# Low parts of streamed weight pieces: one engine before, two engines after

## The chip, the core and the metric

The kernel runs on one core of a Trainium2 chip. The metric is the time of one execution on the device in microseconds (us). Five engines work side by side, each through its own instructions in a fixed order: TensorE (PE in the profile; PEld is its loading of weights), VectorE (DVE), ScalarE (ACT), GpSimd (POOL) and SyncE (SP, which only issues DMAs here). They wait for each other by semaphores.

## What is computed

Two layers of a hybrid backbone over 256 latent tokens with 256 context tokens, width 1024. Cut to what matters here:

```python
for l in range(2):
    u = rms_norm(h, norm1_g[l]) * (1 + sc1) + sh1          # h: 256 latent (+ 256 context) tokens x 1024
    a_x, a_g, b_q, b_f, b_i, b_o, c_qkv, m_g = split_projection(u @ w_in[l])
    ya = rglru_branch(a_x, a_g, ...)                       # gated linear recurrence, both directions
    yb = hgrn2_branch(b_q, b_f, b_i, b_o, ...)             # state-expanded recurrence, both directions
    yc = neighbourhood_attention(c_qkv, ...)
    h = h + gt1 * (sum_n sigmoid(m_g[n]) * (y_n @ w_branch[l, n])) @ w_out[l]
    h = h + gt2 * sq_relu(modulated_rms_norm(h) @ ffn_w1[l]) @ ffn_w2[l]
```

The context tokens run through the same weights in layer 0; in layer 1 only what the latent tokens read of them is computed. Everything is float32 in and out.

## The kernel before

**Exact products from two parts.** TensorE multiplies in a rounded format. So each float32 operand is split: a high part (the value rounded, written by ScalarE, line 226) and a low part (the value less its high part, line 227), and each product is three matmuls: high by high, high by low, low by high (`mm3`, lines 240 to 242; `mm3_pairs`, 253 to 255; the token-major pieces, 1027 to 1029).

**Weight pieces.** The weights of a layer lie in DRAM as pieces of 128 x 1024, each 512 KB, and are streamed by SyncE into `raw` (three buffers, line 211). `weights` splits a piece into `whi` (ScalarE) and `wlo` (before: VectorE), four buffers of each:

```python
def weights(l, key, raw=None, eng=nc.vector):
    ...
    split(hi, lo, raw, eng=eng)

def split(hi, lo, src, scale=None, eng=nc.vector):
    if scale is None:
        nc.scalar.copy(hi, src)                                                    # line 226
        eng.tensor_tensor(out=lo, in0=src, in1=hi.bitcast(F32), op=ALU.subtract)   # line 227
```

One piece alone (the first, at the start) already has its low part on GpSimd. `fetch` runs ahead: while a piece is multiplied, up to three more are split. With 512 tokens (layer 0) a piece is 24 matmuls of 512 columns, with 256 tokens (layer 1) 24 of 256 columns.

**The order of the pieces** in a layer: four heads with ten pieces each (four token-major `tok` pieces that are multiplied together, then `ff`, `fb`, `hq`, `ax`, `ag`, `og`; the first head of layer 0 has no streamed `tok`), 24 gates and 12 branch projections, eight output pieces (`out`), then the MLP: `f1` (up) and `f2` (down), 32 pieces each. The first four `f1` pieces of an MLP are `("f1", 0, 0)` to `("f1", 0, 3)`. The queue `todo` counts the streamed pieces from 0: heads, merge and MLP of layer 0 are pieces 0 to 143, those of layer 1 pieces 144 to 291; the first four `f1` are 80 to 83 and 228 to 231.

**Work between the matmuls.** The chains of the three mixers (`hgrn`, `attention`, `lru`) are cut into steps that are issued between runs of matmuls. A step is a few VectorE and ScalarE instructions and then matmuls (`lv` line 547, `sc` 746, `pr` and `pi` 847) that need them. In layer 0 VectorE also computes most of the modulation by products of rows (`junk`, line 354).

**The norms.** Before an MLP, and before layer 1, the new residual `h` (line 1145) is squared and summed (`sums`, line 420), summed over the features by TensorE (`nss`, line 429), turned into a reciprocal root by three single-input VectorE steps and seven steps on two inputs (`r_g`, 128 x 2, lines 488 to 490 and 495), spread by TensorE (`rst`, line 443), and applied chunk by chunk: `ut` (line 459, reads `h` and the PSUM tile `rst`), `xhi` (ScalarE, 462) and `xlo` (VectorE, 463, reads `ut` and `xhi`). The next piece's matmuls need `xhi` and `xlo`.

A list scheduler puts each engine's instructions in a row, by its own estimate of when each could run; so an edit on one engine can move others. At run time each row is run as it stands.

Of the kernel before, what the change touches and what calls it, by code (L numbers as in the profile page):

```python
# [56 lines left out]
def merge_order(l):  # L57
    # some gates first, while the mixers' chains end
    count = {}
    for part in MERGE[l].split():  # L60
        bi = int(part[0])
        for what in part[1:]:
            i = count.get((bi, what), 0)
            count[bi, what] = i + 1
            yield bi, BRANCH_ORDER[bi], {"g": "gate", "p": "proj"}[what], i
# [35 lines left out]
class Piece:  # L101
    """Products with streamed weights: body(weights) yields after each run of products."""
# [5 lines left out]
class Lanes:  # L108
    """Chains of dependent steps that are issued between the runs of products.

    A step yields the time that the vector engine needs for what it issued, and how many runs more the chain waits."""
# [43 lines left out]
def hybrid_kernel(  # L155
# [67 lines left out]
    def split(hi, lo, src, scale=None, eng=nc.vector):  # L223
        # hi <- rounded part of scale * src, lo <- the rest
        if scale is None:
            nc.scalar.copy(hi, src)  # L226
            eng.tensor_tensor(out=lo, in0=src, in1=hi.bitcast(F32), op=ALU.subtract)  # L227
        else:
            nc.scalar.mul(hi, src, scale)
            nc.vector.scalar_tensor_tensor(  # L230
                out=lo, in0=src, scalar=scale, in1=hi.bitcast(F32), op0=ALU.mult, op1=ALU.subtract
            )
# [13 lines left out]
    def mm3_pairs(dsts, ws, x, nk, c0, c1):  # L246
        # two pieces at a time, so that x may still be arriving
        for i in range(0, len(dsts), 2):
            for k in range(nk):
                xhi, xlo = (t[:, c0:c1] for t in x(k))  # L250
                for p_, (whi, wlo) in zip(dsts[i:i + 2], ws[i:i + 2]):
                    d = p_[:, c0:c1]
                    nc.tensor.matmul(d, lhsT=whi[:, k, :], rhs=xhi, start=(k == 0), stop=False)
                    nc.tensor.matmul(d, lhsT=whi[:, k, :], rhs=xlo, start=False, stop=False)
                    nc.tensor.matmul(d, lhsT=wlo[:, k, :], rhs=xhi, start=False, stop=(k == nk - 1))
                if k % 2:
                    yield
# [5 lines left out]
    def layer_scalars():  # L263
# [13 lines left out]
        for l in range(DEPTH):  # L277
            # f = lb + (1 - lb) * (1 + tanh) / 2 as offset and slope
# [40 lines left out]
    def rope_tables(l):  # L319
        # ctab[:, cos|sin, tile, k|q, head, :], with the norm's gains and the scores' scale  # L320
        for sc in range(2):
            for i, qk in enumerate((1, 0)):
                g = gf[l][:, 2 * sc + qk, :]
                for hd in range(2):
                    for tt in range(2):
                        nc.gpsimd.tensor_tensor(out=ctab[:, sc, tt, i, hd, :], in0=cst[:, sc, tt, :], in1=g, op=ALU.mult)

# [1 line left out]
    mod = [cpool.tile([P, 3, 2, 16], F32, name=f"mod{l}") for l in range(DEPTH)]  # L329

    def modulation_rows():
        # most sections, a row for each feature: the vector engine has time while the tensor engine is busy
# [34 lines left out]
    def last_modulation():  # L367
        # the last section: four groups of columns in four parts of the array
# [55 lines left out]
    def column_sums(parts, n, tag="A"):  # L424
        # sums over the features, one column for each 128 tokens
# [12 lines left out]
    def spread(r, n, tag="A"):  # L438
        # a row of n * 128 columns in every partition
# [14 lines left out]
    def modulated(u, r, a, b, k, s):  # L454
        # u = h * r * a + b in high and low parts
# [29 lines left out]
    def small_rstd(ss, n, temps):  # L485
        # 1 / sqrt(ss / n + eps) for a few columns: a first guess from the exponent, two steps
# [6 lines left out]
        # with x = v * r * r: r * (15 - 10 x + 3 x^2) / 8, but for the factor 3 / 8, then r * (3 - x) / 2 with that factor  # L493
# [14 lines left out]
    def first_half():  # L508
        # the latent stream's norm, before its products are issued
# [5 lines left out]
    def hgrn(l, j, TF, Q, vtok, sog, ys):  # L515
# [4 lines left out]
        # products over blocks, states of the context stream  # L520
# [9 lines left out]
        # within blocks of 64 tokens, the blocks of a tile side by side  # L530
# [7 lines left out]
        def place(b, src, shift):  # L538
            # blocks in the upper (b = 0) or the lower half of the partitions
# [13 lines left out]
        def mixed(t, hh, c0, n):  # L553
            # [first halves of slot 0 | second halves of slot 1] of the 2*hh blocks in columns c0..c0+n
# [17 lines left out]
        # A^T[s, t] of both directions, level by level  # L572
        Tt = TF[:]
        width = T2
        for lev in range(8):
# [11 lines left out]
            # widen the products to blocks of 2*hh  # L587
# [30 lines left out]
        # final states of the context stream  # L618
# [18 lines left out]
        # outputs, token-major  # L637
# [34 lines left out]
    def attention(l, j, qk, vtok, bias, ys):  # L672
        Tq = T2 if l == 0 else TL
        misc = two_k("misc")
        # normalised keys and queries, token-major: [k | q] of two heads for each 128 tokens
# [23 lines left out]
        # rotary embedding of the latent tokens  # L699
# [48 lines left out]
        def softmax(qt, sc):  # L748
            # both heads at once
# [55 lines left out]
        def applied(qt):  # L805
            # both heads at once, in two parts of the array
# [87 lines left out]
    def fin_query(Tq, Q, p_):  # L894
        # twice the silu
# [5 lines left out]
    def fin_outgate(l, Tq, sog, p_):  # L901
        # the gain over four times (1 + tanh)
# [17 lines left out]
    def fin_gelu(Tq, ge, p_):  # L920
        # twice the tanh GeLU
# [12 lines left out]
    def mixer_pieces(l):  # L934
        T = T2 if l == 0 else TL
        heads = []
        for j in range(4):
# [9 lines left out]
            def opened(nm, m=m, j=j):  # L947
                # tiles of a chain, when its first piece begins
# [9 lines left out]
                if nm == "tok":  # L958
                    m.bias = four_k("bias", (4, TL))
                    (nc.gpsimd if l or j else nc.sync).dma_start(out=m.bias, in_=biasd[l, j])  # L960
                    # [v of both mixers | k and q], two blocks of tokens each
# [28 lines left out]
            def group(ws, m=m, opened=opened, closed=closed):  # L990
                # the first products, while the modulation arrives
# [70 lines left out]
    def merge_pieces(l):  # L1062
# [7 lines left out]
        def gate_tile(bi, d):  # L1070
            # several gates in a tile
# [78 lines left out]
    def down_pieces(l, kind, sub, x, section, T, finished, after, pre=None):  # L1150
        # pieces d = 0..7 into the residual; with after, the last four by streams, so that a norm can start early
# [119 lines left out]
    def start():  # L1271
# [51 lines left out]
        def busy(n):  # L1323
            # keeps the tensor engine's clock up while the first data arrive
# [30 lines left out]
        def arrive():  # L1355
            # what the products of the first chunk need
# [11 lines left out]
        def later():  # L1368
            # what the products of the first chunks don't need
# [11 lines left out]
        def ahead(k, n):  # L1381
            # within the products of chunk k, what those of chunk k + 2 need
# [24 lines left out]
    # weights run ahead of the pieces that use them  # L1407
# [3 lines left out]

    def fetch(n):
        while len(ready) < n and pos[0] < len(todo):
            l, key = todo[pos[0]]
            ready.append(weights(l, key))
# [146 lines left out]
```

## Time and profile before

| | us |
|---|---|
| median of 3 runs | 1526.16 (1526.15 to 1528.68) |
| span of the profiled execution | 1526.3 |
| TensorE busy in it | 1513.7 (99%) |
| VectorE busy | 1115.9 (73%) |
| ScalarE busy | 735.0 (48%) |
| GpSimd busy | 26.4 (2%) |

The profiled execution has a span of 1526.3 us, 0.1 us above the median of the runs, so what its rows add up to can be set against the median directly. [...] A busy TensorE in this profile is one with matmuls in its pipeline; their ends are modelled, so the distance from the start of one matmul to the start of the next tells its rate, and "idle before" tells where it waited.

### The profile page before, as it was taken

How to read it: one execution, taken by the hardware profiler on the slowest of the kernel's cores; microseconds unless marked ns; L12 is line 12 of the kernel's file. 1: busy time of each engine (PE TensorE's matmuls, PEld its weight loads, DVE VectorE, ACT ScalarE, POOL GpSimd, SP SyncE). 2: the span in 40 equal slices, each digit the busy share in tenths (PEclk: the TensorE clock that was granted, in tenths of full speed). 3: DMA queues.
4: the chain of work that ended last, by engine and by line, in shares of the span. 5: the costliest groups of instructions: out<-in, count | busy, mean ns of one | idle time of the engine just before them, and what ended most of it. 6: DMA issues, size and time to landing. Idle time of an engine off the chain costs nothing.

```text
span 1526.3 us, 24145 instructions
## 1 busy us (share of the span) xinstructions
PE 1513.7 (99%) x9554; PEld 1300.8 (85%) x9554; DVE 1115.9 (73%) x2118; ACT 735.0 (48%) x1229; POOL 26.4 (2%) x57
## 2 busy tenths in 40 slices
PE   9999999999999999999999999999999999999999
PEld 4778788878888889888888889888888899999999
DVE  6776768586478898988685856778787856776664
ACT  3457575666333333532322323475766854454442
POOL 0200000020000000000000000000000000000000
PEclk9999999999999999999999999999999999999999
DMA  9413122221273562445463532313313345755553
GB/s 368 146 53 104 56 90 70 70 77 62 91 250 136 187 240 70 171 174 206 139 220 127 204 126 82 133 63 126 104 70 105 109 167 182 274 167 184 186 183 125
DMA packets 61793, 217.36 MB, mean 142 GB/s; under 512 B 7792, under 2 KB 9456, under 8 KB 61680
## 3 DMA queue, kind: packets, MB, share of 16 engines
q1 hardware_dynamic: 59328, 209.88, 39.5%
q0 software_dynamic: 1648, 5.77, 1.2%
q8 instruction: 75, 1.23, 0.3%
q14 instruction: 38, 0.31, 0.1%
q10 hardware_dynamic: 704, 0.17, 0.1%
HBM read 214.74 MB, written 1.05 MB: 141 GB/s over the span
## 4 chain that ended last, share of the span: by engine, by line
PE 96%; DVE 2%; ACT 1%; issue 1%; DMA 0%; SPq 0%; DVEq 0%
PE pd L240 7%; PE pd L242 7%; PE pd L241 7%; PE pf L242 5%; PE pf L240 5%; PE pf L241 5%; PE pg L240 5%; PE pg L241 4%; PE pg L242 4%; PE ptok L1027 3%; PE ptok L1029 3%; PE ptok L1028 3%; PE lv L547 2%; PE pp L241 2%; PE pp L240 2%; PE pp L242 2%
## 5 line engine op out<-in xcount | busy, mean ns | idle before, releaser
L226 ACT CAST whi<-raw 128x1024 fp32r<-128x1024 f32 x296 | 310.3, 1050 | 477.0 <-PE pd L241 157.2
L227 DVE TENSOR_TENSOR wlo<-raw,whi 128x1024 fp32r<-128x1024 f32 x295 | 360.3, 1223 | 151.2 <-ACT whi L226 149.4
L242 PE MATMUL pd<-hhi,wlo 128*128 128x256 f32 (+1 forms) x544 | 177.8, 327 | 0.0
L240 PE MATMUL pd<-hhi,whi 128*128 128x256 f32 (+1 forms) x544 | 177.8, 327 | 0.0
L241 PE MATMUL pd<-hlo,whi 128*128 128x256 f32 (+1 forms) x544 | 177.7, 327 | 0.0
L354 DVE CUSTOM_DVE_ANT_0 junk<-arow,crow 128x1024 bf16<-128x1024 f32 x144 | 173.3, 1219 | 2.2 <-DMA arow<-in_adaw 2.0
L241 PE MATMUL pf<-xlo,whi 128*128 128x256 f32 (+1 forms) x464 | 155.0, 334 | 0.0
L242 PE MATMUL pf<-xhi,wlo 128*128 128x256 f32 (+1 forms) x464 | 155.0, 334 | 0.0
L240 PE MATMUL pf<-xhi,whi 128*128 128x256 f32 (+1 forms) x464 | 155.0, 334 | 0.0
L240 PE MATMUL pg<-xhi,whi 128*128 128x512 f32 (+1 forms) x384 | 131.5, 342 | 0.0
L241 PE MATMUL pg<-xlo,whi 128*128 128x512 f32 (+1 forms) x384 | 129.2, 336 | 0.0
L242 PE MATMUL pg<-xhi,wlo 128*128 128x512 f32 (+1 forms) x384 | 129.2, 336 | 0.0
L1145 DVE SCALAR_TENSOR_TENSOR h<-pd,mod,h 128x256 f32<-128x256 f32 x120 | 54.9, 480 | 81.2 <-PE pd L242 79.2
L241 PEld LDWEIGHTS pd<-hlo,whi 128*128 128x128 f32 x544 | 103.5, 190 | 8.8
L240 PEld LDWEIGHTS pd<-hhi,whi 128*128 128x128 f32 x544 | 103.5, 190 | 8.8
L242 PEld LDWEIGHTS pd<-hhi,wlo 128*128 128x128 f32 x544 | 103.5, 190 | 8.6
L241 PEld LDWEIGHTS pf<-xlo,whi 128*128 128x128 f32 x464 | 88.1, 190 | 8.8
L242 PEld LDWEIGHTS pf<-xhi,wlo 128*128 128x128 f32 x464 | 88.1, 190 | 8.7
L240 PEld LDWEIGHTS pf<-xhi,whi 128*128 128x128 f32 x464 | 88.0, 190 | 8.7
L1027 PE MATMUL ptok<-whi,xhi 128*128 128x512 f32 (+1 forms) x224 | 87.4, 395 | 1.1 <-DVE h L1145 1.1
L1029 PE MATMUL ptok<-wlo,xhi 128*128 128x512 f32 (+1 forms) x224 | 84.4, 377 | 0.0
L1028 PE MATMUL ptok<-whi,xlo 128*128 128x512 f32 (+1 forms) x224 | 84.2, 376 | 0.2 <-DVE xlo L463 0.2
(329 smaller groups left out, 3240.0 us busy)
## 6 DMA issues: line engine op xcount, KB each, us to landing
raw<-in_wpack SPq DMA_DIRECT2D x296, 512.0 KB, 3.5
arow<-in_adaw SPq DMA_DIRECT2D x72, 512.0 KB, 4.7
a<-in_ada0w SPq DMA_DIRECT2D x16, 512.0 KB, 10.4
araw<-in_lastw SPq DMA_DIRECT2D x8, 512.0 KB, 6.3
bias<-in_biasd POOLq DMA_DIRECT2D x7, 512.0 KB, 4.3
h<-in_xT SPq DMA_DIRECT2D x4, 512.0 KB, 5.5
gw<-in_lruw POOLq DMA_DIRECT2D x8, 256.0 KB, 2.9
out<-h SPq DMA_DIRECT2D x8, 128.0 KB, 2.0
```

The costliest lines, as they stand in the source:

```text
L226: nc.scalar.copy(hi, src)
L227: eng.tensor_tensor(out=lo, in0=src, in1=hi.bitcast(F32), op=ALU.subtract)
L240: nc.tensor.matmul(d, lhsT=whi[:, k, :], rhs=xhi, start=(k == 0), stop=False)
L241: nc.tensor.matmul(d, lhsT=whi[:, k, :], rhs=xlo, start=False, stop=False)
L242: nc.tensor.matmul(d, lhsT=wlo[:, k, :], rhs=xhi, start=False, stop=(k == nk - 1))
L354: nc.vector.tensor_tensor_reduce(out=junk, in0=raw, in1=crow[s], scale=1.0, scalar=0.0, op0=ALU.mult, op1=ALU.add, accum_out=section_of(l, ...
L547: nc.tensor.matmul(dst, lhsT=lhs(b), rhs=rhs(b), start=True, stop=True)
L1027: nc.tensor.matmul(dst, lhsT=xhi[:, k, tsl], rhs=whi[:, kk, :], start=(k == 0), stop=False)
L1028: nc.tensor.matmul(dst, lhsT=xlo[:, k, tsl], rhs=whi[:, kk, :], start=False, stop=False)
L1029: nc.tensor.matmul(dst, lhsT=xhi[:, k, tsl], rhs=wlo[:, kk, :], start=False, stop=(k == KD - 1))
L1145: nc.vector.scalar_tensor_tensor(out=h[:, d, sl], in0=p_[:, sl], scalar=mods(l, section, s)[:, d:d + 1], in1=h[:, d, sl], op0=ALU.mult, op ...
```

## The change

The engine of a low part now depends on the place of its piece in the queue: every second piece, and the first four pieces of each MLP, go to GpSimd. Of 292 streamed pieces those are 146 + 4 = 150. The arithmetic is the same.

```diff
     todo = [key for p in pieces for key in p.keys]
     ready = deque()
     pos = [0]
 
+    def low_part_engine(key, i):
+
+        return nc.gpsimd if i % 2 or (key[0] == "f1" and key[1] == 0 and key[2] < 4) else nc.vector
+
     def fetch(n):
         while len(ready) < n and pos[0] < len(todo):
             l, key = todo[pos[0]]
-            ready.append(weights(l, key))
+            ready.append(weights(l, key, eng=low_part_engine(key, pos[0])))
             pos[0] += 1
```

The rest of the diff drops comments and empty lines. In each head GpSimd gets the second and fourth `tok` piece, `fb`, `ax` and `og`.

On GpSimd the low parts stand between its few other instructions, the table `ctab` and the DMA issues of `gw` and `bias`. This is the piece of the difference from the end of head 2 of layer 0 to that of layer 1's first head:

```order
 L968 DMA gw<-in_lruw 128x512
 L960 DMA bias<-in_biasd 128x1024
+L227 TENSOR_TENSOR wlo<-raw,whi 128x1024 x5
+L968 DMA gw<-in_lruw 128x512
+L227 TENSOR_TENSOR wlo<-raw,whi 128x1024
+L960 DMA bias<-in_biasd 128x1024
+L227 TENSOR_TENSOR wlo<-raw,whi 128x1024 x4
+L326 TENSOR_TENSOR ctab<-cst,gf_74 128x64 x16
+L968 DMA gw<-in_lruw 128x512
+L227 TENSOR_TENSOR wlo<-raw,whi 128x1024 x51
```

GpSimd's row is no longer a few set-up steps but low parts throughout, with the DMA issues among them.

On VectorE, at the norm before layer 1's MLP (`r_g` is the reciprocal root, `ut` and `xlo` the normed input), the row before was:

```order
L227 TENSOR_TENSOR wlo<-raw,whi 128x1024
L1145 SCALAR_TENSOR_TENSOR h<-pd,mod_86,h 128x256
L488 TENSOR_SCALAR r_g_12660<-nss 128x2
L489 TENSOR_SCALAR r_g_12660<-r_g_12660 128x2
L490 TENSOR_SCALAR r_g_12660<-r_g_12660 128x2
L495 SCALAR_TENSOR_TENSOR r_g_12660<-r_g_12660 128x2
L227 TENSOR_TENSOR wlo<-raw,whi 128x1024
L495 SCALAR_TENSOR_TENSOR r_g_12660<-r_g_12660 128x2 x6
L459 SCALAR_TENSOR_TENSOR ut<-h,A_g_12671,rst 128x256 x3
L463 SCALAR_TENSOR_TENSOR xlo<-ut,mod_86,xhi 128x256 x3
```

and it is now:

```order
L1145 SCALAR_TENSOR_TENSOR h<-pd,mod_86,h 128x256
L488 TENSOR_SCALAR r_g_12660<-nss 128x2
L489 TENSOR_SCALAR r_g_12660<-r_g_12660 128x2
L490 TENSOR_SCALAR r_g_12660<-r_g_12660 128x2
L495 SCALAR_TENSOR_TENSOR r_g_12660<-r_g_12660 128x2 x7
L459 SCALAR_TENSOR_TENSOR ut<-h,A_g_12671,rst 128x256 x3
L463 SCALAR_TENSOR_TENSOR xlo<-ut,mod_86,xhi 128x256 x3
```

The two low parts that stood before and inside the chain of `r_g` have left VectorE's row; the chain's own steps are the same and stand together. At the norm before layer 0's MLP three low parts leave in the same way, and at the norm before layer 1 one leaves the chain of `r_g` and one the steps behind it.

## Rows read from the trace of the kernel before

**Rows 1.** The page, busy time of the engines (share, instructions).

```profile
PE 1513.7 (99%) x9554; PEld 1300.8 (85%) x9554; DVE 1115.9 (73%) x2118; ACT 735.0 (48%) x1229; POOL 26.4 (2%) x57
```

**Rows 2.** Who TensorE waited for: us in total, times, longest.

```profile
PE pf L253 <- ACT xhi L462: 2.7, 3, 1.1
```

**Rows 3.** Groups by line and form: busy us, mean ns, idle time before.

```profile
L227 DVE TENSOR_TENSOR wlo<-raw,whi 128x1024 fp32r<-128x1024 f32 x295 | 360.3, 1223 | 151.2 <-ACT whi L226 149.4
...
L227 POOL TENSOR_TENSOR wlo<-raw,whi 128x1024 fp32r<-128x1024 f32 x1 | 2.3, 2342 | 11.4 <-ACT whi L226 11.4
```

**Rows 4.** Timeline at the start: start us, us, engine, line, instruction.

```profile
11.62 0.17 DVE L301 TENSOR_TENSOR lq<-lq,lz 128x16 f32<-128x16 f32 x1
...
11.88 2.34 POOL L227 TENSOR_TENSOR wlo<-raw,whi 128x1024 fp32r<-128x1024 f32 x1 [11.44 <-ACT whi L226]
...
12.03 2.21 DVE L301 TENSOR_TENSOR lq<-lq,lz 128x16 f32<-128x16 f32 x1
```

**Rows 5.** Timeline a little later, VectorE's `ut` under GpSimd's `ctab`.

```profile
42.05 2.08 POOL L326 TENSOR_TENSOR ctab<-cst,gf 128x64 f32<-128x64 f32 x6
...
43.23 0.86 DVE L459 SCALAR_TENSOR_TENSOR ut<-h,A_start,rst 128x256 f32<-128x256 f32 x2
```

**Rows 6.** Busy time by stretch: PE, PEld, DVE, ACT, POOL, PEclk, DMA, GB/s.

```profile
972.00:1240.00 268.00, 268.00 (x1864) 231.66 (x1863) 207.48 (x469) 179.85 (x321) 2.69 (x5) 1.00 0.31 106
1240.00:1326.00 86.00, 86.00 (x719) 86.00 (x718) 60.90 (x101) 42.50 (x68) 0.00 (x0) 1.00 0.61 214
```

**Rows 7.** Timeline at the norm before layer 1's MLP.

```profile
1331.94 1.98 ACT L226 CAST whi<-raw 128x1024 fp32r<-128x1024 f32 x2
...
1333.90 1.23 DVE L227 TENSOR_TENSOR wlo<-raw,whi 128x1024 fp32r<-128x1024 f32 x1
1335.05 1.13 DVE L495 SCALAR_TENSOR_TENSOR r_g<-r_g 128x2 f32<-128x2 f32 x6
...
1336.24 0.43 PE L443 MATMUL rst<-con,r_g 128*128 128x128 f32 x2 [0.33 <-DVE r_g L495]
...
1337.78 0.50 PE L253 MATMUL pf<-xhi,whi 128*128 128x256 f32 x2 [1.11 <-ACT xhi L462]
```

**Rows 8.** Timeline at the norm before layer 0's MLP, first stream.

```profile
589.25 1.05 ACT L226 CAST whi<-raw 128x1024 fp32r<-128x1024 f32 x1 [1.51 <-issue]
...
592.58 1.05 ACT L226 CAST whi<-raw 128x1024 fp32r<-128x1024 f32 x1 [1.96 <-issue]
593.05 0.54 DVE L495 SCALAR_TENSOR_TENSOR r_g<-r_g 128x2 f32<-128x2 f32 x3
...
593.89 0.38 PE L443 MATMUL rst<-con,r_g 128*128 128x128 f32 x2
...
596.21 0.63 PE L253 MATMUL pf<-xhi,whi 128*128 128x256 f32 x3 [0.50 <-ACT xhi L462]
```

**Rows 9.** Timeline at the norm before layer 1, first stream.

```profile
945.54 1.23 DVE L227 TENSOR_TENSOR wlo<-raw,whi 128x1024 fp32r<-128x1024 f32 x1
...
947.09 0.55 DVE L495 SCALAR_TENSOR_TENSOR r_g<-r_g 128x2 f32<-128x2 f32 x3
...
950.72 1.06 ACT L226 CAST whi<-raw 128x1024 fp32r<-128x1024 f32 x1 [0.73 <-ACT xhi L462]
...
952.22 1.69 DVE L463 SCALAR_TENSOR_TENSOR xlo<-ut,mod,xhi 128x256 fp32r<-128x256 f32 x4
...
955.08 0.50 PE L1027 MATMUL ptok<-whi,xhi 128*128 128x512 f32 x1 [1.11 <-DVE h L1145]
```

**Rows 10.** Timeline in a head of layer 1.

```profile
1064.13 0.69 DVE L227 TENSOR_TENSOR lx<-xc,lx 128x512 fp32r<-128x512 f32 x1
...
1065.13 0.85 PE L847 MATMUL pr<-lx,lw 128*128 128x512 f32 x3
```

**Rows 11.** Timeline in layer 1's MLP, TensorE: two matmuls in a row.

```profile
1508.28 0.28 PE L242 MATMUL pd<-hhi,wlo 128*128 128x256 f32 x1
1508.40 0.28 PE L240 MATMUL pd<-hhi,whi 128*128 128x256 f32 x1
```

## The prediction

> **What bounds the kernel now.** I read the busy times first: TensorE has work for 1513.7 of 1526.3 us, VectorE for 73% of the span, GpSimd for 2% [rows 1]. That alone says that freeing VectorE can only help where TensorE stands still, so the second view is the list of TensorE's waits. Behind the start (which the change leaves alone) only the norms are left in it: three waits for `xhi`, 2.7 us together [rows 2], and with them 1.11 us for `h` before layer 1 [rows 9] and 0.33 us for the reciprocal root before layer 1's MLP [rows 7]. Sum 4.1 us. Between them TensorE runs at its own pace: two matmuls of 256 columns start 0.12 us apart [rows 11], so a piece of layer 1 takes 24 x 0.12 = 2.9 us. No shorter path elsewhere can give more than these 4.1 us, and any new wait is added in full.
>
> **What leaves VectorE, what GpSimd takes.** VectorE loses 150 low parts of 1.22 us, 183 us of work. GpSimd needs 2.34 us for the same instruction [rows 3], so it gains 150 x 2.34 = 351 us and is busy for a quarter of the span. In a steady stretch of layer 1 it gets one piece in two, 2.34 us of every 2 x 2.9 = 5.8 us: it keeps up.
>
> **Do the two engines run side by side?** This decides everything, and the trace of before has one place that shows it: the one low part that GpSimd already makes. It runs from 11.88 to 14.22. A VectorE step on 16 columns, `lq`, starts at 12.03 under it and takes 2.21 us, to 14.24; its twin 0.4 us earlier took 0.17 [rows 4]. So that step waited for GpSimd's whole instruction. Both read two tensors from SBUF. VectorE's `ut`, which reads one tensor from SBUF and one from PSUM, shows no such thing: two of them take 0.86 us under a run of GpSimd's `ctab` [rows 5].
>
> [...]
>
> So moving a low part doesn't free 1.22 us; it takes 2.34 us of the time in which VectorE can run its two-input steps, 1.12 us more than before. This is harmless where VectorE has room. From 1240 to 1326 us it is busy for 60.9 of 86 us [rows 6]; about 30 pieces of 2.9 us fall into that stretch, 15 of them moved, and 60.9 + 15 x 1.12 = 77.7 us still fit. It isn't harmless on the norms' chains, where the next step of VectorE is what TensorE waits for. Three places, in order of their simplicity:
>
> *Before layer 1's MLP.* ScalarE finishes two high parts at about 1333.0 and 1333.9 [rows 7], both of the first four `f1`. On GpSimd their low parts run at once, back to back: 1333.0 to 1335.3 and 1335.3 to 1337.7. In these 4.7 us lie the seven two-input steps of `r_g`, which in the trace end at 1336.2 (with one low part of 1.23 us between them). If one step slips in where the first low part ends and six wait for the second, they end at 1337.7 + 1.13 = 1338.8, 2.6 us later; if all seven slip in, at 1335.3 + 1.3 = 1336.6, 0.4 us later. If nothing is held, the chain is 1.2 us shorter, and all of that is TensorE's waiting now (0.33 + 1.11). Nothing behind this place gives anything back. I take +2.5 (from -1.2 to +2.8), since rows 4 show a held step waiting to the end.
>
> *Before layer 0's MLP.* High parts end at 590.3 and 593.6 [rows 8]; the second low part starts at 590.3, ends on VectorE 1.22 us later and on GpSimd 2.34 us later, so `r_g` behind it falls back by 1.1 us; its last three steps, due at 593.05, come to lie under the next hold, 593.6 to 596.0, and end at about 596.5, 2.9 us late. TensorE meets this at `rst` (593.89), which stands in its row ahead of the rest of the output piece, so it waits 2.6 us there and saves the 0.50 us at 596.21. The fourth low part then holds a few `xlo`: up to 1 us more. The second stream's wait of 1.11 us, 14 us later, is covered by then, because VectorE also has a low part less ahead of it. Together +2 (from -1.6 to +3.3).
>
> *Before layer 1.* The piece at 945.5 holds `r_g` to 947.9 where VectorE's own low part ended at 946.8: +1.1 at once, since `rst` is due then. The piece whose high part ends at 951.8 holds the four `xlo` due at 952.2 [rows 9] until 954.1: +1.9, with some slack in `ptok`. The wait of 1.11 us at 955.08 is for an `h` that stands behind those `xlo` in VectorE's row, so it isn't recovered. +2.5 (from -1.1 to +3).
>
> *The eight heads.* 38 moved low parts, each between 0 and 1.12 us: at most 43 us. VectorE idles 268 - 207 = 61 us in layer 1's heads [rows 6], which can swallow holds; but one of the thinnest hand-overs, `lx` to `pr`, has only 0.3 us from the end of `lx` (1064.13 + 0.69 = 1064.82) to the first matmul of `pr` (1065.13) [rows 10]. I take one hold in twenty of that bound, +2 (0 to +10).
>
> *The other stretches* cost nothing: a low part there is made three pieces ahead, 3 x 2.9 - 1.05 (the high part) = 7.6 us, against 1.2 us of waiting for a VectorE step plus 2.34. If that cover were gone, each moved piece would cost its excess. GpSimd's row also holds 15 DMA issues behind which low parts now queue; they wait for buffers, but stand in the row where their buffers should be free.
>
> Sum: 2.5 + 2 + 2.5 + 2 = +9. On the span, 1526.3 + 9 = 1535.3; the median lies 0.1 lower, and I say 1535.
>
> **Rivals.**
>
> *The chain is freed after all.* If GpSimd's low parts hold VectorE's short steps less than the one row shows (say that a waiting step goes first whenever GpSimd has not yet begun to read), the norms lose 1.2, 1.1 and up to 2.4 us of low parts and the heads nothing: TensorE gets back up to its 4.1 us, and the time is about 1522. For it: VectorE's chains do get shorter in the row of instructions. Against: the 2.21 us.
>
> *It cancels.* The holds are there, but the high parts come a little earlier or later than in the trace of before, and most of the low parts fall between the steps, so that a site gains up to its 1.2 us of low part or loses as much. About 1526, within 3 us.
>
> *The heads decide.* If every fourth hold of 1.12 us meets a hand-over as thin as that of `lx` and is passed on to TensorE, the heads cost about 38 x 1.12 / 4 = 11 us, not 2: 1526.3 + 7 + 11 = 1544. It decides from the point at which VectorE's hand-overs in the heads are thinner than a hold.
>
> That the change doesn't do what it says can be left out: GpSimd's row holds the 150 low parts.
>
> **How the numbers follow.** A measurement of this kernel can tell about 0.2%, 3 us. Chances: the forecast (1530 to 1540) 0.57; freed (1522) 0.12; cancels (1523 to 1529) 0.20; the heads decide (1540 and more) 0.11. Faster by over 0.2%: 0.12. Within: 0.20. Slower: 0.57 + 0.11 = 0.68. The range takes in the cancelling case and the lower part of the heads' case: 1523 to 1545, leaving out about half of the first rival (0.06) and less than half of the last.
>
> **What would show it.** In the profile of the changed kernel: low parts on GpSimd of 2.3 to 3.6 us, 150 more of them; short VectorE steps (`r_g` of 128 x 2) with a duration of one to two microseconds in place of 0.15, and their mean over the group up several times, while `ut` stays at 0.47; TensorE's waits for `rst` and `xhi` at the three norms longer, not shorter, the largest before layer 1's MLP; VectorE's busy time down by less than 183 us, because a held step counts as busy. I am wrong if `r_g` runs through under a low part at its old length, or if TensorE's new waits lie in the heads or in the waiting for `wlo` itself.

## The result: slower by 2.6%

The changed kernel takes 1567.4 us (median of four runs, 1562.2 to 1570.0), the kernel before 1526.4 us beside it; the ratio is 1.0255, with a 95% interval from 1.0234 to 1.0276. The prediction said 1535 us, 1523 to 1545. Its sign was right, and the size was wrong by a factor of four to five: 41 us, not 9.

The profiled execution of the changed kernel took 1567.1 us and has a span of 1565.3 us, 39.0 us more than the span before. The first row of its page, to be read against [rows 1], has each engine's busy time, share of the span and number of instructions:

```profile
PE 1525.7 (97%) x9553; PEld 1304.5 (83%) x9554; DVE 1139.5 (73%) x1968; ACT 734.3 (47%) x1229; POOL 405.1 (26%) x207
```

VectorE has 150 instructions less and is busy **longer**, by 1139.5 - 1115.9 = 23.6 us. 150 low parts of 1.22 us (183 us) have left it [rows 3], so its other instructions have become 183 + 24 = 207 us longer. Summed over the trace, what each VectorE instruction took beyond the usual duration of its form gives the same: some 120 instructions were lengthened by 0.1 us or more, by about 204 us together. That is the hold, and the groups by line and form show where it sits (busy us, mean ns, idle before). First the kernel before, one group that had never met a GpSimd low part:

```profile
L1209 DVE TENSOR_TENSOR rl<-rl 128x256 f32<-128x256 f32 x32 | 13.4, 419 | 0.0
```

then the changed kernel, with the two groups of low parts that answer to [rows 3] (... stands for lines left out, here and below):

```profile
L227 POOL TENSOR_TENSOR wlo<-raw,whi 128x1024 fp32r<-128x1024 f32 x151 | 380.1, 2518 | 1121.6 <-ACT whi L226 1089.0 <-PE pf L241 13.5 <-DVE h L1145 7.6
...
L354 DVE CUSTOM_DVE_ANT_0 junk<-arow,crow 128x1024 bf16<-128x1024 f32 x144 | 192.4, 1352 | 0.9 <-DMA arow<-in_adaw 0.4
L227 DVE TENSOR_TENSOR wlo<-raw,whi 128x1024 fp32r<-128x1024 f32 x145 | 189.5, 1307 | 120.0 <-ACT whi L226 119.0
...
L1209 DVE TENSOR_TENSOR rl<-rl 128x256 f32<-128x256 f32 x32 | 41.8, 1307 | 10.5 <-ACT rl L1208 10.5
...
L420 DVE TENSOR_TENSOR sums<-sums,sqt 128x256 f32<-128x256 f32 x34 | 29.1, 869 | 7.7 <-ACT sqt L418 7.7
...
L1145 DVE SCALAR_TENSOR_TENSOR h<-pd,mod,h 128x256 f32<-128x256 f32 x120 | 53.8, 477 | 54.4 <-PE pd L242 53.4 <-PE pd L255 1.0
```

`rl` reads two operands in SBUF and takes three times as long as before (1.31 us on average, not 0.42); `h` reads one of its inputs from PSUM and none of its 120 instructions took over 0.49 us, 13 of them wholly under a low part.

What of the 204 us reaches TensorE stands in its list of waits (us in total, times, longest). It answers to [rows 2], where one line of 2.7 us was the largest:

```profile
PE rst L443 <- DVE r_g L495: 5.8, 3, 2.7
PE tp L793 <- ACT s L769: 5.6, 5, 3.2
PE lv L547 <- DVE km L560: 3.4, 3, 1.1
PE pd L242 <- POOL wlo L227: 3.2, 4, 1.0
PE ptok L1027 <- ACT sog L903: 2.1, 1, 2.1
PE ptok L1028 <- DVE xlo L463: 1.7, 2, 1.5
...
PE pf L254 <- DVE xlo L463: 1.5, 1, 1.5
PE pd L253 <- ACT mhi L229: 1.4, 1, 1.4
...
PE pd L241 <- DVE mlo L230: 0.8, 1, 0.8
```

By stage, from the times at which the first matmul of a piece starts in the two traces:

| stage (pieces) | before, us | after, us | more | foretold |
|---|---|---|---|---|
| start and first head, to piece 6 | 95.7 | 96.1 | 0.4 | |
| heads 2 to 4 of layer 0 (6 to 35) | 237.5 | 242.8 | 5.3 | heads: 2 in all |
| first gates, in which head 4's chains end (36 to 47) | 85.4 | 90.4 | 5.0 | |
| other gates and projections (48 to 71) | 131.5 | 131.5 | 0 | 0 |
| output pieces and norm before the MLP (72 to 87) | 93.6 | 100.0 | 6.4 | 2 |
| MLP of layer 0, norm before layer 1, its first head (88 to 153) | 357.5 | 360.4 | 2.9 | 2.5 |
| heads 2 to 4 of layer 1 (154 to 183) | 187.3 | 193.9 | 6.6 | |
| first gates (184 to 199) | 61.6 | 64.2 | 2.6 | |
| other gates and projections (200 to 219) | 57.6 | 57.6 | 0 | 0 |
| output pieces and norm before the MLP (220 to 239) | 65.3 | 69.7 | 4.4 | 2.5 |
| MLP of layer 1 (240 on) | 153.3 | 158.7 | 5.4 | 0 |

The column adds up to the 39 us. About 26 us of them are waits of TensorE above 0.1 us (30.2 us behind the first 60 us of the span, against 4.4 before), and some 7 us are a lower granted clock behind such waits (below). The remaining 6 us stand in the profile as busy time of TensorE, whose ends of matmuls are modelled; waits under 0.1 us are only 0.3 us in all. In two rows part of the loss lies ahead of the norm: 1.4 of the 6.4 us at the first output piece of layer 0, and 2.3 of the 4.4 us at the first two of layer 1.

**A wait at one remove.** The longest, 3.2 us for `tp`, is not a wait for VectorE by its name. The timeline of the changed kernel in the first gates of layer 0 (start us, us, engine, line, instruction, idle before and who ended it):

```profile
339.32 2.40 POOL L227 TENSOR_TENSOR wlo<-raw,whi 128x1024 fp32r<-128x1024 f32 x1 [11.96 <-ACT whi L226]
339.44 2.83 DVE L594 TENSOR_TENSOR KK<-KK,blk 128x512 f32<-128x512 f32 x1
...
343.12 0.15 DVE L760 SCALAR_TENSOR_TENSOR misc<-misc 128x2 f32<-128x2 f32 x1
...
343.37 0.69 ACT L764 ACTIVATE s<-sc,misc 128x512 f32<-128x512 f32 x1 [4.13 <-DVE misc L760]
...
346.06 1.12 PE L793 MATMUL tp<-con,s 128*128 128x128 f32 x4 [3.25 <-ACT s L769]
```

`KK`, 0.69 us long elsewhere, starts 0.12 us behind a low part on GpSimd and takes 2.83 us. Everything behind it in VectorE's row comes some 2 us late, `misc` among it, on which the softmax on ScalarE waits, on which TensorE waits.

**What a wait costs beyond itself.** Behind four of the longer waits (2.05, 3.25, 2.65 and 1.86 us) the granted clock falls from 1.00 to 0.50 for 3.41 us. Busy time by stretch of the changed kernel (us, then PE, PEld, DVE, ACT and POOL busy with instructions, PEclk, DMA share, GB/s), two of the four and last, at full clock, the stretch that follows the first of them:

```profile
345.83:349.24 3.41, 3.19 (x12) 2.81 (x13) 1.65 (x6) 2.06 (x5) 0.00 (x0) 0.50 0.00 0
...
1369.83:1373.24 3.41, 3.34 (x17) 3.10 (x15) 3.41 (x10) 2.36 (x6) 0.00 (x0) 0.50 0.01 4
349.24:352.65 3.41, 3.41 (x38) 2.59 (x36) 0.81 (x2) 2.76 (x5) 0.00 (x0) 1.00 0.00 0
```

In the stretch from 608.65 us on, matmuls of 256 columns start 0.21 us apart, right behind it 0.12. If half the granted clock is half the work, 3.41 us do the work of 1.7, and the four cost up to 6.8 us: an estimate from the two figures of the granted clock. In the trace of before the granted clock is 1.00 from 38 us to the end. In the prediction no term stands for this. The same wait isn't followed by the lower clock each time: in the trace of run 4 the 2.65 us before layer 0's MLP are not (its mean granted clock is 0.999, as before the change), and in that of run 3 (0.996) the waits of 1.27 and 1.50 us before layer 1, which the changed kernel has too, are followed by 6.83 us of it.

### The profile page after: what moved, and what is told of

It reads as the page before. It is cut to its first block, busy times and chain, and to the rows that moved or that the text cites. A ratio compares the mean times of both kernels' runs of the same rounds, so it can differ in the third digit from the quotient of the medians.

```text
span 1565.3 us, 24161 instructions
## 1 busy us (share of the span) xinstructions
PE 1525.7 (97%) x9553; PEld 1304.5 (83%) x9554; DVE 1139.5 (73%) x1968; ACT 734.3 (47%) x1229; POOL 405.1 (26%) x207
## 4 chain that ended last, share of the span: by engine, by line
PE 74%; DVE 17%; ACT 5%; issue 2%; DMA 1%; POOL 1%; SPq 0%; ACTq 0%; DVEq 0%
PE pd L242 6%; PE pd L241 6%; PE pd L240 6%; PE pg L240 4%; PE pg L241 4%; PE pg L242 4%; PE pf L240 3%; PE pf L241 3%; PE pf L242 3%; ACT whi L226 3%; PE ptok L1027 3%; PE ptok L1029 3%; PE ptok L1028 3%; DVE wlo L227 2%; DVE rl L1209 2%; PE pp L242 2%
## 5 line engine op out<-in xcount | busy, mean ns | idle before, releaser
L227 POOL TENSOR_TENSOR wlo<-raw,whi 128x1024 fp32r<-128x1024 f32 x151 | 380.1, 2518 | 1121.6 <-ACT whi L226 1089.0
L227 DVE TENSOR_TENSOR wlo<-raw,whi 128x1024 fp32r<-128x1024 f32 x145 | 189.5, 1307 | 120.0 <-ACT whi L226 119.0
L354 DVE CUSTOM_DVE_ANT_0 junk<-arow,crow 128x1024 bf16<-128x1024 f32 x144 | 192.4, 1352 | 0.9 <-DMA arow<-in_adaw 0.4
L1209 DVE TENSOR_TENSOR rl<-rl 128x512 f32<-128x512 f32 (+1 forms) x64 | 90.1, 1409 | 23.3 <-ACT rl L1208 23.3
L226 ACT CAST hhi<-rl 128x512 fp32r<-128x512 f32 (+1 forms) x64 | 32.9, 514 | 129.9 <-DVE rl L1209 129.9
```

The source lines that it names most:

```text
L354: nc.vector.tensor_tensor_reduce(out=junk, in0=raw, in1=crow[s], scale=1.0, scalar=0.0, op0=ALU.mult, op1=ALU.add, accum_out=section_of(l, ...
L1209: nc.vector.tensor_mul(rl, rl, rl)
```

## Experiments

All ratios are to the kernel before, run on the same chip beside them. The edits are shortened to what matters.

**1. GpSimd writes, but reads nothing.** TensorE's row is that of the changed kernel, VectorE's differs in two places.

```diff
-eng.tensor_tensor(out=lo, in0=src, in1=hi, op=ALU.subtract)
+if eng is nc.gpsimd and pos[0]:
+    eng.memset(lo, 0.0)
+else:
+    eng.tensor_tensor(out=lo, in0=src, in1=hi, op=ALU.subtract)
```

> In the 150 moved pieces GpSimd writes zeros into the low part in place of subtracting (the low parts of these pieces are left out of the products). Rows of TensorE are the same as in the changed kernel, VectorE's differ in two places, but GpSimd reads nothing from SBUF. Theory (GpSimd's reads of SBUF hold VectorE's two-input steps): about 1524 us (1521 to 1530), `rl` back from 1.41 us to about 0.55, VectorE busy about 940 us. Rival, the changed order of the rows is what costs: 1560 to 1567 as in the changed kernel. Rival, GpSimd hands the low parts over too late: in between, 1555 to 1565 if the zeros take as long as the subtraction, with TensorE waiting for `wlo`.

Measured: 1524.35 us, ratio 0.9983 (0.9971 to 0.9996). The page's busy times and two groups of this kernel (in it line 1209 is line 1212):

```profile
PE 1512.9 (99%) x9554; PEld 1299.7 (85%) x9554; DVE 951.5 (63%) x1968; ACT 736.8 (48%) x1229; POOL 170.0 (11%) x207
```

```profile
L1212 DVE TENSOR_TENSOR rl<-rl 128x256 f32<-128x256 f32 x32 | 13.5, 422 | 11.7 <-ACT rl L1211 11.7
```

```profile
L228 POOL MEMSET wlo<- 128x1024 f32 x150 | 143.1, 954 | 1299.2 <-PE pd L245 276.9 <-PE pg L245 213.2 <-PE pf L245 210.5
```

The rows of instructions as the change makes them are not to blame: with the same rows and no reads the kernel is a little faster than before. `rl` is back at 0.42 us. This also tells what VectorE's relief is worth without the hold: 0.17% (0.04 to 0.29), some 2.6 us, within the 4.1 us of the prediction's list of recoverable waits. One thing is less sharp: the zeros take 0.95 us and not 2.34, so GpSimd is also earlier here than in the changed kernel. That is what the next run excludes.

**2. The hold without the relief.** VectorE keeps all its low parts; GpSimd computes the 150 once more into a tile that nobody reads.

```diff
+spare = cpool.tile([P, 1024], mybir.dt.float8e4, name="spare")
 ready.append(weights(l, key))
+if i % 2 or (key[0] == "f1" and key[1] == 0 and key[2] < 4):
+    nc.gpsimd.tensor_tensor(out=spare, in0=raw, in1=whi, op=ALU.subtract)
```

> VectorE computes every low part as before the change; GpSimd computes the 150 low parts once more into a tile that nobody reads. Theory (the hold): slower than the changed kernel's 1567, since VectorE keeps its 183 us of work and is held besides: 1570 to 1610, VectorE busy above 1250 us. Rival, the order of rows: 1526 to 1530. Rival, late low parts: 1526 to 1530, since no consumer waits for GpSimd.

Measured: 1623.8 us, ratio 1.0628 (1.0602 to 1.0653). Page and GpSimd's group:

```profile
PE 1547.0 (96%) x9554; PEld 1314.9 (81%) x9554; DVE 1365.8 (84%) x2118; ACT 732.5 (45%) x1229; POOL 479.2 (30%) x207
```

```profile
L1421 POOL TENSOR_TENSOR spare<-raw,whi 128x1024 fp8e4<-128x1024 f32 x150 | 451.3, 3008 | 1086.6 <-ACT whi L229 926.4 <-issue 140.8 <-DVE aux L493 10.7
```

The rows of TensorE, VectorE and ScalarE are those of the kernel before. No consumer waits for these low parts, so neither a late low part nor a changed order can be the cause here; VectorE does the work of before and is busy 250 us longer. The time is above the theory's range (1570 to 1610). The copies take 3.0 us each instead of 2.5, and a raw buffer comes free later too, which this run doesn't separate.

**3. Every second piece only** (`i % 2` without the rule for the first four of an MLP).

> Only every second piece goes to GpSimd, without the first four pieces of each MLP (146 of the 150). Theory (holds everywhere): 1556 to 1567, since 146 of 150 holds stay and the two places before the MLPs cost about 11 us of the 41. Rival, the rule for the first four pieces is what costs: 1530 to 1550.

Measured: 1567.0 us, ratio 1.025 (1.0225 to 1.0274), the same as the changed kernel. The two places before the MLPs cost a little less here (3.9 and 3.5 us by the starts of the pieces, against 6.4 and 4.4), and other places a little more: in the first head of layer 1, whose first pieces wait for the norm's `xlo`, 4.6 us instead of 1.8, where the granted clock is 0.50 for 6.8 us, twice as long as at any place in the changed kernel.

**4. The first four of each MLP only** (8 pieces).

> Only the first four pieces of each MLP go to GpSimd (8 pieces), the rest stays on VectorE. Theory: 1526 to 1534, the holds at the two norms alone; the two places lost about 11 us in the changed kernel, part of it by odd pieces that stay on VectorE here. If the chain is freed here and the odd pieces did the harm there: 1523 to 1526. Rival, this rule is what costs: 1545 or more.

Measured: 1537.4 us, ratio 1.0057 (1.0038 to 1.0076), some 9 us, above the theory's range. Eight low parts cost a fifth of what 150 do. The profiled execution is the shortest of the six, 1534.1 us with a mean granted clock of 0.999; the other five have 0.993 to 0.998, so a part of the 9 us is lower clock that this trace doesn't show. The timeline at the norm before layer 1's MLP, the place of [rows 7]:

```profile
1334.99 4.67 POOL L227 TENSOR_TENSOR wlo<-raw,whi 128x1024 fp32r<-128x1024 f32 x2 [0.50 <-ACT whi L226]
1335.47 1.92 DVE L489 TENSOR_SCALAR r_g<-r_g 128x2 int32<-128x2 int32 x1
1337.42 2.26 DVE L490 TENSOR_SCALAR r_g<-r_g 128x2 int32<-128x2 int32 x1
1339.72 1.33 DVE L495 SCALAR_TENSOR_TENSOR r_g<-r_g 128x2 f32<-128x2 f32 x7
...
1341.11 0.69 PE L443 MATMUL rst<-con,r_g 128*128 128x128 f32 x2 [4.01 <-DVE r_g L495]
```

The held steps are not those that the prediction counted. `L489` and `L490` have **one** input, 128 x 2, and each waits to the end of a low part (1337.39 and 1339.68). Two short steps in a row cost two whole holds, and the wait of 0.33 us [rows 7] became 4.01 us.

**5 and 6. The heads alone, and all the rest alone.**

```diff
+heads = key[0] in ("tok", "ff", "fb", "hq", "ax", "ag", "og")
-eng = gpsimd if i % 2 or first_four else vector
+eng = gpsimd if i % 2 and heads else vector                     # run 5
+eng = gpsimd if (i % 2 or first_four) and not heads else vector # run 6
```

> The odd pieces of the eight heads go to GpSimd, all other low parts stay on VectorE. Theory: the losses of the changed kernel add up by stage (heads there: 10.4 us in layer 0, 11.0 us in layer 1, by the times at which the pieces start), so 1526 + 21 = 1547 us (1540 to 1553). Rival, the heads cost 2 us as in the prediction: 1526 to 1531.

> The odd pieces of merge, output and MLP and the first four of each MLP go to GpSimd; in the heads all low parts stay on VectorE. Theory: the other half of the loss, 1526 + 18 = 1544 us (1538 to 1551), of which some 5 in layer 1's MLP. Rival (the heads are the cause): 1526 to 1535.

Measured: heads 1543.5 us, 1.0098 (1.0083 to 1.0114); rest 1549.4 us, 1.0136 (1.0122 to 1.015). Together 2.34%, against 2.55%: the losses add up by place. The split is 15 to 21 and not 21 to 18, because the losses in the first gates belong to the pieces of those gates (layer 0: 85.4 us in run 5 as before, 89.4 in run 6; layer 1: 61.8 and 64.1): their low parts hold the last head's chains. And the low parts of layer 1's first head hold the norm ahead of it: that row of the table is 5.8 us longer in run 5, with 6.83 us at a granted clock of 0.50 in it (the mean of that execution is 0.997, against 0.999 before), and unchanged in run 6. A low part harms the chains that run while it is made, whatever piece it is for.

**7. Holds of half the length.** Each GpSimd low part in two instructions of 512 columns.

> The changed kernel with each GpSimd subtraction cut into two of 512 columns: same work, each hold half as long, and a step of VectorE can run between them. [...]

Measured: 1556.7 us, ratio 1.0179 (1.0165 to 1.0193): the loss falls from 2.55% to 1.79%, by less than a third, though one GpSimd instruction takes 1.48 us on average and not 2.52. Layer 1's MLP waits for no low part any more, and the longest hand-overs get a little shorter (1.1 us for `lv` became 0.8). But the wait for `tp` is 2.9 us still. Its timeline:

```profile
334.81 2.99 POOL L230 TENSOR_TENSOR wlo<-raw,whi 128x512 fp32r<-128x512 f32 x2 [11.85 <-ACT whi L226]
335.05 1.60 DVE L597 TENSOR_TENSOR KK<-KK,blk 128x512 f32<-128x512 f32 x1
...
336.91 1.44 DVE L601 TENSOR_TENSOR QQ<-QQ,blk 128x512 f32<-128x512 f32 x1
```

`KK` waits for the first half, `QQ` two steps later for the second. Over the whole trace some 200 instructions are held instead of some 120, for about 165 us instead of 204. By this timeline what counts is how much of the holding a row of dependent steps meets, and two halves meet most of it; no run tests that by itself.

**8. Steps that aren't held, at the norms.** On the kernel of run 4, every step of the reciprocal root reads one input from PSUM; what would be used twice is made twice.

```diff
-times(t, r, 1.0, ALU.mult, r)
-times(t, t, 1.0, ALU.mult, v)
+times(w, r, 1.0, ALU.mult, rs)      # w, r, t in PSUM; rs, vs, ts in SBUF
+for o in (t, ts):
+    times(o, w, 1.0, ALU.mult, vs)
...
```

> The kernel with the first four pieces of each MLP on GpSimd (1537 us), and at the three norms each step of the reciprocal root now reads one of its inputs from PSUM (what is used twice is made twice: 15 steps for 10, some 0.8 us more). Theory: a step with one input in PSUM isn't held, so TensorE's waits for the spread root (2.65 and 4.01 us) fall under 1 us each: 1527 to 1532 us. Rival, the chain is late because its sums come late: 1537 to 1541.

Measured: 1531.4 us, ratio 1.0024 (1.0014 to 1.0033), against 1.0057 of run 4. The norm before layer 1's MLP again:

```profile
1340.54 4.69 POOL L227 TENSOR_TENSOR wlo<-raw,whi 128x1024 fp32r<-128x1024 f32 x2 [0.55 <-ACT whi L226]
...
1341.16 0.17 DVE L494 TENSOR_SCALAR nss<-nss 128x2 int32<-128x2 int32 x1
1341.37 0.17 DVE L496 TENSOR_SCALAR nss<-nss 128x2 int32<-128x2 int32 x1
...
1341.76 0.37 DVE L491 SCALAR_TENSOR_TENSOR nss<-nss,r_g 128x2 f32<-128x2 f32 x2
```

Under the same two low parts back to back the same steps run through at 0.16 to 0.19 us. TensorE's wait for `rst` is 0.13 us here, not 4.01 (1.07 us instead of 2.65 before layer 0's MLP). Of what is left, 2.3 us lie at the norm before layer 1, near which no low part is on GpSimd: that is the price of the added steps.

**9. The same cure for `rl`.** The changed kernel with one operand of `rl`'s square in PSUM; TensorE's row is unchanged.

```diff
-nc.vector.tensor_mul(rl, rl, rl)
+nc.vector.scalar_tensor_tensor(out=rl, in0=p_[:, :T], scalar=0.0, in1=rl, op0=ALU.max, op1=ALU.mult)
```

> The changed kernel, with the square of `rl` (line 1209) computed from the PSUM tile and `rl` in place of `rl` and `rl`; TensorE's row is the same. Theory: `rl` is no longer held, ScalarE's `hhi` and the next high part behind it come in time again, and TensorE's waits for `wlo` in layer 1's MLP (four of about 1 us) go: about 1561 us (1558 to 1563), `rl` at 0.4 to 0.8 us instead of 1.41. Rival, a low part of 2.34 us is simply too slow for layer 1's pieces: the waits stay, 1565 to 1570.

Measured: 1562.3 us, ratio 1.0221 (1.0206 to 1.0236). The waits for `wlo` in layer 1's MLP are gone; its pieces 240 to 259 take 57.6 us as before the change, not 61.4. The two groups that matter in this kernel:

```profile
L227 DVE TENSOR_TENSOR hlo<-rl,hhi 128x256 fp32r<-128x256 f32 x32 | 32.0, 1001 | 14.3 <-ACT hhi L226 14.3
...
L1209 DVE SCALAR_TENSOR_TENSOR rl<-pf,rl 128x256 f32<-128x256 f32 x32 | 13.4, 419 | 10.4 <-ACT rl L1208 10.4
```

The hold has moved to the next two-input step, `hlo` (0.42 us before), where TensorE doesn't feel it. So it was not the length of GpSimd's instruction that made low parts late, but the ring that `rl` closed. The changed kernel there:

```profile
1413.99 2.38 POOL L227 TENSOR_TENSOR wlo<-raw,whi 128x1024 fp32r<-128x1024 f32 x1 [4.73 <-ACT whi L226]
1414.22 2.43 DVE L1209 TENSOR_TENSOR rl<-rl 128x256 f32<-128x256 f32 x1 [0.81 <-ACT rl L1208]
...
1416.69 0.41 ACT L226 CAST hhi<-rl 128x256 fp32r<-128x256 f32 x1 [2.50 <-DVE rl L1209]
1417.00 1.05 ACT L226 CAST whi<-raw 128x1024 fp32r<-128x1024 f32 x1
...
1421.11 2.37 POOL L227 TENSOR_TENSOR wlo<-raw,whi 128x1024 fp32r<-128x1024 f32 x1 [4.74 <-ACT whi L226]
...
1423.53 0.39 PE L242 MATMUL pd<-hhi,wlo 128*128 128x256 f32 x1 [1.03 <-POOL wlo L227]
```

The low part on GpSimd holds `rl`; ScalarE's `hhi` waits for `rl`; the next `whi` stands behind `hhi` in ScalarE's row; the next low parts wait for that `whi`. One turn takes 1421.11 - 1413.99 = 7.1 us and yields two pieces, which TensorE multiplies in 5.8. The cover of three pieces is used up in a few turns, and then each turn costs TensorE about 1 us.

**10. Only where nothing was lost.** 34 odd pieces, among 48 to 71, 88 to 111 and 200 to 219.

> Only the odd ones of the pieces 48 to 71, 88 to 111 and 200 to 219 go to GpSimd (34 pieces: stretches in which the changed kernel lost nothing), the rest stays on VectorE. Theory: the holds are there (VectorE busy about as before, since 34 x 1.22 us go and some 20 to 45 us of holding come), but no hand-over in them is thin: 1525 to 1529, no change, and no gain either. Rival, each hold costs: 34 x 1.12 = 38 us at most, 1535 or more.

Measured: 1528.3 us, ratio 1.0001 (0.9992 to 1.0009). VectorE is busy for 1112.5 us, 3 less than before, though 34 x 1.22 = 41 us have left it: the holds took 38 back. They cost TensorE nothing there, and nothing is won.

**11. The norms' cure in the changed kernel.**

> The changed kernel, with the three norms' reciprocal roots reading one input from PSUM in each step (15 steps for 10). Theory: TensorE's waits for the spread root (2.65, 1.27 and 1.86 us) and the two drops of the granted clock behind them go or shrink, less some 0.8 us for the added steps: 1559 to 1564 us. Rival, the waits stay: 1566 to 1571.

Measured: 1569.2 us, ratio 1.0263 (1.0246 to 1.0281): a miss. Before the two MLPs the waits for the spread root fell as foretold (2.65 to 1.07 us, 1.86 to 0.13), but before layer 1 it rose (1.27 to 1.52), behind it the wait for `xlo` grew from 1.51 to 1.80, another for `xlo` (1.19) is new, one for `xhi` (1.11) stands in place of that for `h`, and there are two stretches of 3.41 us at a granted clock of 0.50. The longer chain also changed TensorE's row of instructions. Run 8, where no low part on GpSimd lies near this norm, has one of these waits too (1.11 us for `xhi`), so part of it comes with the added steps; how much of the rest is order and how much is the hold on `xlo` stays open.

**12. One input instead of two.** GpSimd multiplies the raw piece by zero into the low part. The edit is against run 1.

```diff
-eng.memset(lo, 0.0)
+eng.tensor_scalar_mul(lo, src, 0.0)
```

> In the 150 moved pieces GpSimd multiplies the raw piece by zero into the low part: one input from SBUF in place of two (the low parts of these pieces are left out of the products). TensorE's row is that of the changed kernel. Theory, any read of SBUF by GpSimd holds VectorE's two-input steps for as long as it runs: with an instruction of 1.0 to 1.7 us the loss is a fifth to a half of the 41 us, 1530 to 1550, and VectorE's steps show durations up to that length. Rival, only a GpSimd instruction with two inputs holds them: 1522 to 1527, as with zeros written without a read.

Measured: 1529.3 us, ratio 1.0014 (1.0002 to 1.0026). Neither expectation has it right. The instruction is longer than the subtraction, 2.89 us on average in place of 2.52, and still it loses only some 5 us against run 1 (0.31%). The timeline shows why:

```profile
1370.71 2.77 POOL L228 TENSOR_SCALAR wlo<-raw 128x1024 fp32r<-128x1024 f32 x1 [2.98 <-PE pf L245]
1370.76 1.27 DVE L230 TENSOR_TENSOR hlo<-rl,hhi 128x256 fp32r<-128x256 f32 x1 [0.47 <-ACT hhi L226]
1371.99 0.42 DVE L1212 TENSOR_TENSOR rl<-rl 128x256 f32<-128x256 f32 x1
```

`hlo`, 0.42 us long, ends at 1372.03: it was held until 0.90 us after the start of GpSimd's instruction, and `rl` runs through under the other two thirds. At another place a low part of 2.77 us starts at 333.54: `QQ` (0.69 us long elsewhere) was held until 0.89 us after that start, a copy (`km`, 0.42 us elsewhere) that starts 1.91 us after it until 2.63 us. This run also speaks against late low parts, from the other side than run 2: GpSimd takes longer here than for the subtraction, and the loss is 0.14%.

## Why the prediction was wrong

**TensorE is the bound, and at most 4.1 us can be won: right.** Run 1, the change without the hold, gains some 2.6 us.

**The exchange of work: right for VectorE's time, wrong for a chain.** "Takes 2.34 us of the time in which VectorE can run its two-input steps, 1.12 us more than before" gives 150 x 1.12 = 168 us if every low part meets a VectorE that has work. Measured, VectorE's busy time grew by 23.6 us: many low parts fell into its idle time. That it had room, and that holds in idle time are free, run 10 confirms: 0 us for 34 pieces. But a chain doesn't pay 1.12 us. The low part that GpSimd makes at 339.32 stood behind `KK` in VectorE's row before (`KK` at 331.90, the low part at 334.31); on GpSimd it makes `KK` 2.1 us late.

**The hold: right, shown by runs 1 and 2** (ratio 0.9983 where GpSimd reads nothing, 1.0628 where it reads and nobody waits for it). That steps with one input in PSUM are not held is right too for those that were seen: in the changed kernel `h` took at most 0.49 us and `ut` at most 0.48, in run 8 the steps of the root took 0.16 to 0.19 under two low parts, in run 9 `rl` 0.42 on average. What failed is the class of held steps. The sum counted "the seven two-input steps of `r_g`"; two one-input steps on integers before them were held as well, in run 4 each for some 2 us, and so was a copy between SBUF tiles (`km`, 2.65 us at 79.84 of the changed kernel, 0.42 elsewhere). Not every step within SBUF was held: the changed kernel has a reduction that runs through under a low part at its usual 0.69 us, and right behind it a one-input step, 0.17 us elsewhere, that waits to the end of it:

```profile
57.94 2.40 POOL L227 TENSOR_TENSOR wlo<-raw,whi 128x1024 fp32r<-128x1024 f32 x1 [9.95 <-ACT whi L226]
...
58.42 0.69 DVE L686 TENSOR_REDUCE misc<-sq 128x8 f32<-128x512 f32 x1 [1.75 <-ACT sq L685]
59.14 1.23 DVE L488 TENSOR_SCALAR misc<-misc 128x16 f32<-128x16 f32 x1
```

What sets the held one-input steps apart from the reduction no trace here tells. That a step waits for GpSimd's whole instruction the subtraction agrees with to 0.13 us (held steps start some 2.27 us after it, of 2.40), and run 12 doesn't: 0.90 us of 2.77.

**The three norms: +2.5, +2 and +2.5 foretold, 2.1, 5.0 and 2.9 measured** (before layer 1's MLP, before layer 0's, before layer 1), without the output pieces ahead of them. The chains named were the right ones: in the changed kernel the waits for `rst` are 1.86, 2.65 and 1.27 us. Before layer 0's MLP 2.6 us were foretold for `rst`, and up to 1 us for a held `xlo`, which took 1.5; most of what is above the bound is the lower clock behind the wait, 1.7 us. Before layer 1 the waits for `rst` and `xlo` (1.27 and 1.51 us) are close to the 1.1 and 1.9 us of the working. Before layer 1's MLP the waits grew by 0.4 us only (1.86 in place of 0.33 and 1.11) and the lower clock makes up the rest: that the sum fits there is luck. In run 4 they grew by 2.6 us, as foretold.

**The eight heads, +2 (one hold in twenty): the step that failed.** They cost 5.3 + 5.0 + 6.6 + 2.6 = 19.5 us with the gates in which their last chains end, of the bound of 43: nearly one half, not a twentieth. 3.4 of the 19.5 us are lower clock behind two waits, and some 7 come from low parts of the gates' own pieces (runs 5 and 6), which the prediction had put among the other stretches. The bound was none, since it counts 1.12 us for each low part and a chain can meet the whole hold (2.1 us at `KK`, at 339.44). The rival "the heads decide" had the mechanism and one in four. The error lies in looking at one hand-over (`lx` to `pr`, 0.3 us of slack, where TensorE waits 0.2 us a head) and spreading the rest by judgement. The steps that decide are `KK` (2.83 us at 339.44 and 2.21 us at 1023.87, instead of 0.69) and `misc` (2.35 us at 176.74, instead of 0.16), at the head of chains through VectorE and ScalarE that carry a delay on: `lv` waits 1.1 us in each of three heads of layer 1.

**The other stretches, 0: wrong for two of them.** 5.4 us in layer 1's MLP. "A low part there is made three pieces ahead" counted the time that a low part may take, but not whether ScalarE's row can still run ahead when `hhi` in it waits for a held step. GpSimd's load (2.34 of 5.8 us) was looked at, the turn of the ring (7.1 us) was not. And 3.7 us at the first output pieces of both layers, where VectorE's `msum` or `mlo` is held; the changed kernel in layer 1:

```profile
1339.77 2.50 POOL L227 TENSOR_TENSOR wlo<-raw,whi 128x1024 fp32r<-128x1024 f32 x1 [4.92 <-ACT whi L226]
...
1340.61 2.29 DVE L1114 TENSOR_TENSOR msum<-msum,gt 128x256 f32<-128x256 f32 x2
...
1343.06 0.38 PE L253 MATMUL pd<-mhi,whi 128*128 128x256 f32 x1 [1.36 <-ACT mhi L229]
```

In the other stretches 0 was right. The 15 DMA issues behind low parts in GpSimd's row don't show: no wait above 0.1 us in TensorE's list behind the first 60 us ends on a DMA.

**What was not in the sum at all:** up to 6.8 us of lower clock behind four waits, half of it in the heads and half at the norms.

**The signs to look for.** Low parts of 2.3 to 3.4 us, short steps of one to two microseconds, `ut` at 0.47: seen. "VectorE's busy time down by less than 183 us": it went up by 23.6. The waits in the heads and the waits for `wlo`, named as what would prove the prediction wrong, are both there.

## What to carry to other kernels

Before work goes from VectorE to GpSimd, count the reads from SBUF: in this kernel a GpSimd subtraction of two SBUF operands stopped VectorE's two-operand steps, and its copies and one-input arithmetic between SBUF tiles, until it ended (2.4 us). So GpSimd's time is paid in VectorE's: in run 10 41 us left VectorE and 38 came back. Steps with an operand in PSUM escaped it (`h` at 0.49 us or less, `rl` at 0.42 in run 9), and so did the reductions of line 686 (0.69 us). Then take VectorE's chains one by one and let each meet one whole hold at its first step, following the delay through the rows of the other engines (ScalarE's above all) to TensorE; a cover of several pieces counts only if the row that builds it doesn't wait for a held step. A chain that couldn't bear it was cured here by an operand in PSUM (in run 8 the wait for `rst` fell from 4.01 to 0.13 us, in run 9 `rl` from 1.31 to 0.42), at the price of a few steps that can themselves be late (run 11, 1.27 us became 1.52); in run 10 low parts made where VectorE has room cost nothing and, with TensorE as the bound, brought nothing.

## What the runs showed of the hardware beyond expectation

- Some one-input steps from SBUF to SBUF were held: `L489` on 128 x 2 integers took 1.92 us, and 0.17 us from PSUM under the same load (runs 4 and 8); a copy between SBUF tiles of 128 x 512 (`km`, line 560), 0.42 us elsewhere, took up to 2.65 in the changed kernel. Reductions from SBUF (line 686, 128 x 512) kept their 0.69 us under low parts, at 58.42 and 297.08.
- GpSimd's multiplication with one SBUF input held the two-input steps `hlo` and `QQ` for the first 0.90 and 0.89 of its 2.77 us only (run 12, at 1370.71 and 333.54); the subtraction with two inputs held VectorE's steps for 2.27 of 2.40 (changed kernel); under the writing of zeros with no input (0.95 us) `rl` kept its 0.42 us on average (run 1).
- On GpSimd the one-input multiplication of 128 x 1024 took longer, 2.77 us (run 12), than the two-input subtraction, 2.34 us [rows 3].
- TensorE's wait of 1.9 to 3.3 us was followed by a granted clock of 0.50 for 3.41 us at four places of the changed kernel, which adds up to 1.7 us to the wait by the estimate above; in run 4 a wait of 2.65 us was not.
